# A chain of chunk states as one whole-array product for both heads, and small products set side by side in a decoder layer

## The chip, the cores and the metric

The kernel runs on one core of a Trainium2 chip. The metric is device time in microseconds (us) of one execution. A core has five engines that matter here: PE (matrix products; PEld is its loading of the stationary operand), DVE and ACT (elementwise work), POOL (small elementwise work) and SP (which only issues transfers). Each works through its own queue in order and waits for the others by semaphores.

## What is computed

One layer of a hybrid decoder on 512 tokens with 16 "meta" tokens ahead, 1024 channels, 16 heads of 64: sliding-window attention with sinks, beside it an RWKV-7 time mixing, the two merged by gates, a layer norm, a squared-ReLU MLP and a last norm. What matters for the change is the recurrence of the time mixing, per head with a 64x64 state S:

```
def step(S, inp):
    r_t, w_t, k_t, v_t, kk_t, a_t = inp
    sa = einsum('bhij,bhj->bhi', S, -kk_t)
    S = S * w_t[:, :, None, :] + sa[..., None] * (kk_t * a_t)[:, :, None, :] + v_t[..., None] * k_t[:, :, None, :]
    return S, einsum('bhij,bhj->bhi', S, r_t)
_, y = lax.scan(step, S0, (r, w, k, v, kk, a))
...
merged = sigmoid(gate_att) * att + sigmoid(gate_rwkv) * rw
h = layer_norm(ALPHA * h + merged @ w_out, ln1_g, ln1_b)
ff = square(relu(h @ w_ff1)) @ w_ff2
h = layer_norm(ALPHA * h + ff, ln2_g, ln2_b)
```

## The kernel before

Everything large is a dense product of float32 data that is split into a high and a low part (`whi`, `wlo`, `hhi`, `hlo`), so that three fast products (lines 340 to 342, tile `dps`) stand for one. A weight column block arrives by a transfer (`wraw`), ACT casts it to `whi` (line 256) and DVE subtracts to `wlo` (line 259). After the first norm come the input projections, 128 columns at a time, then the output projection (lines 1259 to 1261, tile `o`), then the MLP (lines 340 to 342 again, and 1485 to 1487, tile `acc`).

The 16 heads are taken as 8 pairs, one head in partitions 0 to 63 and the other in 64 to 127. The tokens of a pair are cut into 8 chunks of 64, and the recurrence becomes small float32 products: scores within a chunk (`sc`, line 658), an inverse that is built up block by block (`up`, lines 808, 817, 832, 842), its product with the keys (`wp`, line 859), the fold of everything that acts on the incoming state into one matrix per chunk (`gq`, line 876, added to `AX` by DVE at line 881), and then the chain: 7 steps in which chunk c's state is multiplied to give chunk c+1's. A step (`rwkv_chain`, line 936) was two products, one per head, each with 64 columns of the stationary operand `AX` and the 64 columns of that head's state `Z`, written to two different PSUM tiles (`ch`, `ch2`). `follow` then scales the two results by the chunk's decay into the next `Z`: head 0 on DVE (line 892), head 1 on ACT (line 894). The outputs of all chunks (`Y`, line 950) and their norm (`yt`, line 968) come behind the chain. The attention of a pair is scores (`sp`, line 1099; `copy_predicated`, bias and maximum on DVE, eight exponentials and eight scalings on ACT), transposes (`pt`, line 1143, copied to `pall` by ACT and `pown` by DVE) and the product with the values (`av`, line 1163). Low-rank products (`lps`, line 483), sums of squares (`ss`, line 564), gates (`gp`, line 1085), turned keys (`tr`), scores (`axt`) and values (`vt`) complete a pair.

All of this is laid between the dense products by hand. PE's order is that in which the code issues its instructions; the other engines' instructions are put in order by the framework, with priorities (`ahead`). The program goes through ten slots, one pair further each time: slot s does the scan preparation of pair s (`scan`), the solve and chain of pair s-1 (`solve`), the projections of pair s+1 (`project_in`), the attention of pairs s-1 and s-2 (`attend`, `attend_out`, `join`). Each item of a slot has a number, the time in us of dense work after which it is to come; `weave` sorts the items by it and issues dense products in portions of three (line 340 to 342) until the number is reached. PSUM tiles with the tag "a" (`sp`, `pt`, `av`, `lps`, `ss`, `gp`, `scm`, `bp`) share two banks, those with the tag "g" (`sc`, `axt`, `tr`, `vt`, `wp`, `gq`) two others, "ch" and "Y" one each, the dense products two.

Of the kernel before, what the change touches and what calls it, by code (L numbers as in the profile page):

```python
# [11 lines left out]
F32 = mybir.dt.float32  # L12
# [8 lines left out]
P = 128  # L21
# [7 lines left out]
HD = 64  # L29
C = 64  # L30
NCH = SEQ // C
PAIRS = HEADS // 2
# [98 lines left out]
def hybrid_layer_kernel(ctx: ExitStack, tc: tile.TileContext, I: dict, out: bass.AP):  # L131
# [12 lines left out]
    @contextmanager  # L144
    def ahead(n):

        now = tc.cur_priority
        tc.cur_priority = now - n
        yield
        tc.cur_priority += n  # L150
# [439 lines left out]
    def rwkv_bonus(j):  # L590
        S = SS[j]
        rkh, rkl = S["rk"]
        S["bv"] = dr.tile([P, SEQ], F32, name=f"bv{j}")
        bp = pat.tile([P, 512], F32, name="bp", tag="a")
        pe.matmul(bp, bones, rkh, start=True, stop=False)
        pe.matmul(bp, bones, rkl, start=False, stop=True)
        bv = ew.tile([P, SEQ], F32, name="bv", tag="rk")
        dve.tensor_tensor(bv, bp, S["v"][:, NMETA:], op=ALU.mult)
        nc.sync.dma_start(S["bv"], bv)
# [286 lines left out]
    def follow(S, c, src, last):  # L886

        Z, PC = S["Z"], S["PC"]
        for e in range(2):
            dst, scale = Z[c][ER[e], e, :], PC[ER[e], last : last + 1]  # L890
            if e == 0:
                dve.tensor_scalar(dst, src[e][ER[e]], scale, None, op0=ALU.mult)
            else:
                act.activation(dst, src[e][ER[e]], AF.Copy, scale=scale)  # L894
# [29 lines left out]
    def rwkv_chain(j, c):  # L924

        S = SS[j]
        Z, GQ = S["Z"], S["AX"]
        if c == 0:
            ch = pch.tile([P, 512], F32, name="ch", tag="ch", bufs=PS[2])

            ch2 = pch.tile([P, 512], F32, name="ch2", tag="Y", bufs=PS[3])
            S["st"] = [[b[:, d * C : (d + 1) * C] for b in (ch, ch2)] for d in range(NCH)]
        st = S["st"]
        with ahead(PRI["chain"]):
            for e in range(2):
                pe.matmul(st[c][e][ER[e]], GQ[:, c, 0, e, :], Z[c][:, e, :], start=True, stop=True)  # L936
            follow(S, c + 1, st[c], c)

    def rwkv_outputs(j):

# [413 lines left out]
    def scan(j):  # L1354

        need = (f"k{j}", f"r{j}", f"v{j}")
        return [
            (0.0, need, F(rwkv_scores, j, 0)),
            (3.2, (), F(rwkv_meta, j)),
            (3.2, (), F(rwkv_scores, j, 1)),  # L1360
            (3.2, (), F(rwkv_inverse, j)),
            (6.4, (), F(rwkv_bonus, j)),
            (12.55, (), F(rwkv_turn_scores, j)),
            (18.6, (), F(rwkv_turn_keys, j)),
            (16.0, (), F(rwkv_inverse_place, j)),
            (23.2, (), F(rwkv_turn_values, j)),
        ]

    def solve(j):

        return [
            (0.0, (), F(rwkv_blocks, j, 0)),
            (0.0, (), F(rwkv_start, j, 0)),
            (1.4, (), F(rwkv_blocks, j, 1)),
            (1.4, (), F(rwkv_start, j, 1)),
            (3.2, (), F(rwkv_blocks, j, 2)),
            (3.2, (), F(rwkv_start, j, 2)),
            (4.6, (), F(rwkv_blocks, j, 3)),
            (6.4, (), F(rwkv_turn_inverse, j)),
            (8.4, (), F(rwkv_fold, j, 0)),  # L1380
            (10.6, (), F(rwkv_fold, j, 1)),
        ] + [(11.6 + 0.95 * c, (), F(rwkv_chain, j, c)) for c in range(NCH - 1)] + [
            (18.6, (), F(rwkv_outputs, j)),
            (23.2, (), F(rwkv_norm, j)),
        ]

    def project_in(j):
        return [
            (0.0, (), F(rwkv_begin, j)),
            (8.4, (), F(rwkv_lora, j, 0)),  # L1390
            (10.6, (), F(rwkv_lora, j, 1)),
            (25.5 if j == 1 else 18.6, (f"k{j}",), F(rwkv_sums, j)),
        ]

    def attend(j, t0):
        return [
            (t0, (f"q{j}",), F(attention_scores, j, 0)), (t0 + 2.85, (), F(attention_scores, j, 1)),
        ]

    def attend_out(j, t0, t1, t2):  # L1400
        return [
            (t0, (), F(attention_turn, j, 0)),
            (t1, (), F(attention_out, j, 0)),
            (t1, (), F(attention_turn, j, 1)),
            (t2, (f"ga{j}",), F(attention_out, j, 1)),
        ]

    def join(j, t0, t1, t2):
        return [
            (t0, (f"gr{j}",), F(gate_out, j)), (t1, (), F(merge_rwkv, j)), (t2, (), F(merge, j)),  # L1410
        ]

    with tc.manual_schedule(engines={mybir.EngineType.PE}):
        for s in range(-1, PAIRS + 1):
            if s <= PAIRS:
                units[:] = [u for u in all_units[: marks[s + 1]] if u[0] not in finished]
            items = []
            if s > 0:
                items += solve(s - 1)
            if 0 <= s < PAIRS:  # L1420
                items += scan(s)
            if s == -1:
                items += [
                    (0.0, (), F(rwkv_begin, 0)),
                    (9.0, ("wa",), F(rwkv_lora, 0, 0)),
                    (10.4, (), F(rwkv_lora, 0, 1)),
                    (20.0, ("k0",), F(rwkv_sums, 0)),
                ]
            if 0 <= s < PAIRS - 1:
                items += project_in(s + 1)  # L1430
            if s == 0:
                items += [(18.0, ("av",), F(aside_heads, 0))]
            if s == 4:
                items += [(26.0, (), F(aside_heads, 1))]
            if s in (1, 5):
                items += [(8.6, (), turn_heads)]
            if 0 < s < PAIRS - 1:
                items += attend(s - 1, 12.55) + join(s - 1, 11.6, 25.4, 0)[:2]
            if 1 < s < PAIRS:

                items += attend_out(s - 2, 0.0, 4.6, 6.4) + join(s - 2, 0, 0, 7.0)[2:]
            if s == PAIRS - 1:
                items += [(10.0, (), merged_before)]
                items += attend(s - 1, 10.0) + attend_out(s - 1, 20.5, 22.9, 25.3)
                items += join(s - 1, 11.6, 26.5, 26.5)
                items += attend(s, 16.5)
                items += [(27.2, (), F(load_out, q, 0)) for q in range(3)]
            if s == PAIRS:
                items += attend_out(s - 1, 3.0, 5.4, 7.8) + join(s - 1, 0.0, 24.5, 25.5)
                items += [(2.0, (), F(merged, s - 2)), (25.6, (), F(merged, s - 1))]  # L1450
                items += [(3.0, (), residual_gain), (17.0, (), first_up)]
                items += [(3.0 + 3 * b, (), F(residual_rows, b)) for b in range(4)]
            weave(items, True)
# [261 lines left out]
```

## Time and profile before

| | |
|---|---|
| median of the runs | 972.86 us (971.6 to 973.08, 3 runs) |
| the profiled execution | 971.71 us, of which 969.9 us lie between its first and last instruction |
| busy share of the span | PE 97%, PEld 80%, DVE 65%, ACT 46%, POOL 5% |
| dense input projections and slots | about 60 to 580 us |
| MLP and end | about 580 to 970 us |

The page gives busy time, the span in 40 slices, the transfers, the chain of work that ended last, and groups of instructions with what they waited for. A timeline lists one engine's instructions in order of time: start, duration, engine, line, operation, tiles, rows*columns of the array that it uses, shape and count, and in brackets how long the engine was idle before it and who ended that. Matrix products are pipelined: the listed duration overlaps the next instruction, so what a product costs is read from the distance between starts.

### The profile page before, as it was taken

What the parts mean: (1) busy time and instruction counts of PE and PEld (TensorE: products, weight loads), DVE (VectorE), ACT (ScalarE), POOL (GpSimd) and SP (SyncE); (2) the same over time, 40 slices, a digit from 0 to 9 for tenths busy, and PEclk for the clock granted to TensorE, in tenths of its full rate; (3) what the DMA queues carried; (4) which work ended last, traced back from release to release, by engine and by line L of the source; (5) the groups of instructions that cost most, each with busy time, mean ns of one, the idle gap of its engine ahead of it and who ended that gap; (6) DMA issues with size and microseconds to landing.
All of it is one profiled execution on the core that took longest, in us unless ns stands there. A gap on an engine that the chain in (4) does not pass through costs nothing.

```text
span 969.9 us, 19424 instructions
## 1 busy us (share of the span) xinstructions
PE 942.1 (97%) x7805; PEld 775.6 (80%) x7805; DVE 633.1 (65%) x1444; ACT 447.7 (46%) x1111; POOL 44.3 (5%) x106
## 2 busy tenths in 40 slices
PE   4999999999999999999999999999999999999996
PEld 4888878788797887887876777988888888888885
DVE  8577788787887878868876948575423244542427
ACT  6536357475483664735727635643411224432220
POOL 2001000010000100000001000000000000000001
PEclk9999999999999999999999999999999999999999
DMA  7545323233322323142433725134223232232222
GB/s 271 94 126 129 85 70 93 65 75 91 91 81 82 92 78 92 47 118 74 129 93 90 234 88 216 55 121 130 87 88 107 88 107 90 86 106 90 83 91 87
DMA packets 79650, 99.95 MB, mean 103 GB/s; under 512 B 47174, under 2 KB 54072, under 8 KB 79560
## 3 DMA queue, kind: packets, MB, share of 16 engines
q1 hardware_dynamic: 78064, 96.63, 33.9%
q10 hardware_dynamic: 1496, 2.08, 0.6%
q8 instruction: 61, 1.00, 0.4%
q14 instruction: 29, 0.24, 0.1%
HBM read 85.23 MB, written 13.47 MB: 102 GB/s over the span
## 4 chain that ended last, share of the span: by engine, by line
PE 89%; DVE 5%; ACT 2%; DMA 2%; issue 1%; POOL 1%; SPq 0%; DVEq 0%; ACTq 0%; POOLq 0%
PE dps L340 17%; PE dps L341 15%; PE dps L342 15%; PE acc L1485 6%; PE acc L1486 6%; PE acc L1487 6%; PE av L1163 2%; PE sp L1099 2%; PE o L1259 2%; PE sc L658 2%; PE gq L876 2%; PE ch L936 1%; PE o L1260 1%; PE o L1261 1%; PE wp L859 1%; DVE wlo L259 1%
## 5 line engine op out<-in xcount | busy, mean ns | idle before, releaser
L259 DVE TENSOR_TENSOR wlo<-wraw,whi 128x512 fp32r<-128x512 f32 x240 | 157.1, 685 | 175.0 <-ACT whi L256 174.5
L256 ACT CAST whi<-wraw 128x512 fp32r<-128x512 f32 x240 | 139.8, 617 | 264.8 <-PE dps L341 117.5
L340 PE MATMUL dps<-hhi,whi 128*128 128x264 f32 (+1 forms) x640 | 218.5, 341 | 1.1 <-ACT whi L256 1.0
L341 PE MATMUL dps<-hlo,whi 128*128 128x264 f32 (+1 forms) x640 | 203.6, 318 | 0.9 <-DVE hlo L321 0.9
L342 PE MATMUL dps<-hhi,wlo 128*128 128x264 f32 (+1 forms) x640 | 203.1, 317 | 0.2 <-DVE wlo L259 0.2
L340 PEld LDWEIGHTS dps<-hhi,whi 128*128 128x128 f32 x640 | 120.4, 188 | 25.3 <-issue 14.6
L341 PEld LDWEIGHTS dps<-hlo,whi 128*128 128x128 f32 x640 | 120.8, 189 | 8.9 <-DVE hlo L321 1.7
L342 PEld LDWEIGHTS dps<-hhi,wlo 128*128 128x128 f32 x640 | 120.5, 188 | 8.8 <-DVE wlo L259 0.4
L341 PE MATMUL dps<-h1lo,whi 128*128 128x512 f32 (+1 forms) x256 | 97.3, 380 | 0.0
L340 PE MATMUL dps<-h1hi,whi 128*128 128x512 f32 (+1 forms) x256 | 97.3, 380 | 0.0
L342 PE MATMUL dps<-h1hi,wlo 128*128 128x512 f32 (+1 forms) x256 | 97.3, 380 | 0.0
L341 PEld LDWEIGHTS dps<-h1lo,whi 128*128 128x128 f32 x256 | 48.0, 188 | 10.3
L342 PEld LDWEIGHTS dps<-h1hi,wlo 128*128 128x128 f32 x256 | 48.0, 188 | 10.2
L340 PEld LDWEIGHTS dps<-h1hi,whi 128*128 128x128 f32 x256 | 48.0, 187 | 10.2
L1485 PE MATMUL acc<-whi,hhi 128*128 128x512 f32 x128 | 50.6, 395 | 0.0
L1486 PE MATMUL acc<-wlo,hhi 128*128 128x512 f32 x128 | 50.4, 394 | 0.0
L1487 PE MATMUL acc<-whi,hlo 128*128 128x512 f32 x128 | 50.2, 392 | 0.0
L1485 PE MATMUL acc<-whi,fhi 128*128 128x512 f32 x112 | 43.6, 389 | 0.0
L1486 PE MATMUL acc<-wlo,fhi 128*128 128x512 f32 x112 | 43.6, 389 | 0.0
L1487 PE MATMUL acc<-whi,flo 128*128 128x512 f32 x112 | 43.6, 389 | 0.0
L1585 DVE TENSOR_TENSOR rl<-rl 128x512 f32<-128x512 f32 (+1 forms) x36 | 22.7, 632 | 14.9 <-ACT hhi L1584 9.0
L894 ACT ACTIVATE Z<-ch,PC 64x64 f32<-64x64 f32 x56 | 17.3, 309 | 32.1 <-PE ch L936 31.3
(277 smaller groups left out, 1647.9 us busy)
## 6 DMA issues: line engine op xcount, KB each, us to landing
wraw<-in_w_ff_dram SPq DMA_DIRECT2D x64, 512.0 KB, 3.5
wraw<-in_w_in_dram SPq DMA_DIRECT2D x52, 512.0 KB, 3.6
wraw<-in_w_out_dram SPq DMA_DIRECT2D x8, 512.0 KB, 4.2
xt<-in_x_dram SPq DMA_DIRECT2D x4, 512.0 KB, 6.1
Nd<-NT SPq DMA_DIRECT2D x16, 128.0 KB, 2.9
bv<-bv SPq DMA_DIRECT2D x8, 256.0 KB, 2.7
bvm<-bv SPq DMA_DIRECT2D x8, 256.0 KB, 5.0
XB<-xtd SPq DMA_DIRECT2D x16, 128.0 KB, 3.2
```

Source lines behind the costliest of these rows:

```text
L256: act.copy(hi[:n, qs], raw[:n, qs])
L259: dve.tensor_tensor(lo[:n, qs], raw[:n, qs], hi[:n, qs].bitcast(F32), op=ALU.subtract)
L340: pe.matmul(ps, whi, xhi, start=first, stop=False)
L341: pe.matmul(ps, whi, xlo, start=False, stop=False)
L342: pe.matmul(ps, wlo, xhi, start=False, stop=last)
L658: pe.matmul(scs[d][to, c * P : (c + 1) * P], BK[ER[e], 4 * i + c, to], AXg[ER[e], e, 4 * i + c], start=True, stop=True,)
L876: pe.matmul(gqs[e][:, c * P : (c + 1) * P], WT[ER[e], 4 * i + c, :], GR[ER[e], 4 * i + c, :], start=True, stop=True,)
L1099: pe.matmul(sps[e][:, d * 256 : (d + 1) * 256], q[ER[e], n * P : (n + 1) * P], kk[ER[e], n * P : n * P + 256], start=True, stop=True,)
L1485: pe.matmul(acc[b], xhi[k][:, bs], hi[:, ws], start=first, stop=False)
L1486: pe.matmul(acc[b], xhi[k][:, bs], lo[:, ws], start=False, stop=False)
L1487: pe.matmul(acc[b], xlo[k][:, bs], hi[:, ws], start=False, stop=last)
L1585: dve.tensor_tensor(r, r, r, op=ALU.mult)
```

## The change

A chain step becomes one product for both heads: the stationary operand is all 128 columns of the chunk's `AX` (both heads), the moving one all 128 columns of `Z` (both heads), and the result is a 128x128 block. For each head `Z` holds the state in one half of the partitions and the chunk's values in the other, so that each head's product has all 128 rows, before as now; of the 128x128 result only the two diagonal 64x64 blocks are used, by `follow`. Four steps' results lie side by side in one PSUM tile: steps 0 to 3 in the "ch" tile, 4 to 6 in the "Y" tile, so that DVE's and ACT's halves of one step now stand in the same tile.

The numbers in the slots' lists are changed. Partial-array products (products that use 64 or fewer rows or columns of the array) of different origin now directly follow each other: the low-rank products `lps` come right behind `sc` and behind the meta step at the slot's start (they stood behind the two `gq` groups), attention scores behind the last block of the inverse and before `wp`, the value products `av` behind the two `gq` groups, the outputs `Y` behind `ss`. Chain steps begin earlier (10.4 in place of 11.6) and lie 1.25 apart in place of 0.95. The attention of a pair thereby moves: scores from 12.55 to 4.6, the transposes and value products of the pair before from 0.0 to 6.4 to 7.6 to 10.6. The start of a pair's low-rank work (`rwkv_begin`, a transfer of `lw`) is issued at the end of the slot before, and `bp` moves from the "a" banks to the "g" banks and a little earlier.

```diff
-        bp = pat.tile([P, 512], F32, name="bp", tag="a")
+        bp = pg.tile([P, 512], F32, name="bp", tag="g")
...
         if c == 0:
-            ch = pch.tile([P, 512], F32, name="ch", tag="ch", bufs=PS[2])
-            ch2 = pch.tile([P, 512], F32, name="ch2", tag="Y", bufs=PS[3])
-            S["st"] = [[b[:, d * C : (d + 1) * C] for b in (ch, ch2)] for d in range(NCH)]
-        st = S["st"]
+            S["ch"] = [
+                pch.tile([P, 512], F32, name="ch", tag=t, bufs=PS[b]) for t, b in (("ch", 2), ("Y", 3))
+            ]
+        ps = S["ch"][c // 4][:, c % 4 * P : (c % 4 + 1) * P]
         with ahead(PRI["chain"]):
-            for e in range(2):
-                pe.matmul(st[c][e][ER[e]], GQ[:, c, 0, e, :], Z[c][:, e, :], start=True, stop=True)
-            follow(S, c + 1, st[c], c)
+            pe.matmul(
+                ps, GQ[:, c, 0].rearrange("p e t -> p (e t)"), Z[c].rearrange("p e i -> p (e i)"),
+                start=True, stop=True,
+            )
+            follow(S, c + 1, [ps[:, e * HD : (e + 1) * HD] for e in range(2)], c)
...
-            (6.4, (), F(rwkv_bonus, j)),
+            (5.6, (), F(rwkv_bonus, j)),
...
-        ] + [(11.6 + 0.95 * c, (), F(rwkv_chain, j, c)) for c in range(NCH - 1)] + [
-            (18.6, (), F(rwkv_outputs, j)),
-            (23.2, (), F(rwkv_norm, j)),
+        ] + [(10.4 + 1.25 * c, (), F(rwkv_chain, j, c)) for c in range(NCH - 1)] + [
+            (18.61 + 0.6 * last, (), F(rwkv_outputs, j)),
+            (24.6 - 1.4 * last, (), F(rwkv_norm, j)),
...
-            (0.0, (), F(rwkv_begin, j)),
-            (8.4, (), F(rwkv_lora, j, 0)),
-            (10.6, (), F(rwkv_lora, j, 1)),
+        t0, t1 = (8.4, 10.6) if j == 1 else (0.0, 1.4)
+        begin = [(26.0, (f"k{j}",), F(rwkv_begin, j + 1))] if j < PAIRS - 1 else []
+        return begin + [
+            (t0, (), F(rwkv_lora, j, 0)),
+            (t1, (), F(rwkv_lora, j, 1)),
...
-                items += [(8.6, (), turn_heads)]
+                items += [(2.4, (), turn_heads)]
...
-                items += attend(s - 1, 12.55) + join(s - 1, 11.6, 25.4, 0)[:2]
+                items += attend(s - 1, 4.6, 1.8) + join(s - 1, 13.5, 25.4, 0)[:2]
...
-                items += attend_out(s - 2, 0.0, 4.6, 6.4) + join(s - 2, 0, 0, 7.0)[2:]
+                items += attend_out(s - 2, 7.6, 8.4, 9.4, 10.6) + join(s - 2, 0, 0, 11.6)[2:]
...
-                items += attend(s - 1, 10.0) + attend_out(s - 1, 20.5, 22.9, 25.3)
+                items += attend(s - 1, 4.6, 1.8) + attend_out(s - 1, 15.6, 16.6, 16.6, 18.0)
...
-                items += attend(s, 16.5)
+                items += attend(s, 11.6, 2.2)
```

Three places show what this does to the queues; the rows are the built programs' order, with the shape of the result and a count.

First, PE in the middle of a slot, in the chain. `axt` is the turning of the scores, `sp` the attention scores. Before:

```order
L936 MATMUL ch<-Z,AX 64x64
L936 MATMUL ch_3488<-Z,AX 64x64
L694 MATMUL axt<-con,AX 128x128 x8
L1099 MATMUL sp<-kk,q 128x256 x4
L340 MATMUL dps<-hhi,whi 128x264
```

and now:

```order
L694 MATMUL axt<-con,AX 128x128 x8
L340 MATMUL dps<-hhi,whi 128x264
L341 MATMUL dps<-hlo,whi 128x264
L342 MATMUL dps<-hhi,wlo 128x264
L936 MATMUL ch<-Z,AX 128x128
```

The two products of a step are one, the turning stands by itself between dense products, and the attention scores have left the chain.

Second, PE at the fold (`gq`) ahead of the chain. Before:

```order
L876 MATMUL gq<-GR,WT 128x128 x8
L483 MATMUL lps<-zz,lw 128x264 x2
L340 MATMUL dps<-hhi,whi 128x512
L341 MATMUL dps<-hlo,whi 128x512
L342 MATMUL dps<-hhi,wlo 128x512
```

and now:

```order
L342 MATMUL dps<-hhi,wlo 128x512
L936 MATMUL ch<-Z,AX 128x128
L876 MATMUL gq<-GR,WT 128x128 x8
L1166 MATMUL av<-pall,vtok 64x128 x2
L1166 MATMUL av<-pown,vdif 64x128 x2
```

The low-rank products behind the fold have given way to the value products, and the first chain step stands ahead of the second half of the fold. The low-rank products now stand in the run of small products at the slot's start, behind `sc`, and behind the meta step.

Third, ACT between the later chain steps, with what each instruction waits for (`Z<-ch` is ACT's half of `follow`). Before:

```order
L894 ACTIVATE Z<-ch_4359,PC 64x64 [waits PE_49] x3
L256 CAST whi<-wraw 128x512 [waits DMAHW0_49,PE_49]
L421 ACTIVATE k<-dps,drv 128x264 [waits PE_49]
L256 CAST whi<-wraw 128x512
L894 ACTIVATE Z<-ch_4359,PC 64x64 [waits PE_49]
```

and now:

```order
L894 ACTIVATE Z<-ch,PC 64x64 [waits DVE_49] x2
L256 CAST whi<-wraw 128x512 [waits DMAHW1_49,PE_49]
L421 ACTIVATE k<-dps,drv 128x264 [waits PE_49]
L894 ACTIVATE Z<-ch,PC 64x64 [waits DVE_49]
L256 CAST whi<-wraw 128x512
```

ACT's half of a step waited for PE's product; now, with both halves in one PSUM tile, it waits for DVE's half.

More of the change, by code (lines that the diff above doesn't have):

```diff
@@ L1369, in solve @@
     def solve(j):
+        last = j == PAIRS - 1
         return [
@@ L1381, in solve, with attend, attend_out @@
             (10.6, (), F(rwkv_fold, j, 1)),
-        ] + [(11.6 + 0.95 * c, (), F(rwkv_chain, j, c)) for c in range(NCH - 1)] + [
-            (18.6, (), F(rwkv_outputs, j)),
-            (23.2, (), F(rwkv_norm, j)),
+        ] + [(10.4 + 1.25 * c, (), F(rwkv_chain, j, c)) for c in range(NCH - 1)] + [
+            (18.61 + 0.6 * last, (), F(rwkv_outputs, j)),
+            (24.6 - 1.4 * last, (), F(rwkv_norm, j)),
         ]
     def project_in(j):
-        return [
-            (0.0, (), F(rwkv_begin, j)),
-            (8.4, (), F(rwkv_lora, j, 0)),
-            (10.6, (), F(rwkv_lora, j, 1)),
+        t0, t1 = (8.4, 10.6) if j == 1 else (0.0, 1.4)
[3 more added lines that the diff above has]
+            (t1, (), F(rwkv_lora, j, 1)),
             (25.5 if j == 1 else 18.6, (f"k{j}",), F(rwkv_sums, j)),
         ]
-    def attend(j, t0):
+    def attend(j, t0, dt=3.6):
         return [
-            (t0, (f"q{j}",), F(attention_scores, j, 0)), (t0 + 2.85, (), F(attention_scores, j, 1)),
+            (t0, (f"q{j}",), F(attention_scores, j, 0)), (t0 + dt, (), F(attention_scores, j, 1)),
         ]
-    def attend_out(j, t0, t1, t2):
+    def attend_out(j, t0, t1, t2, t3):
         return [
@@ L1403, in attend_out @@
             (t1, (), F(attention_out, j, 0)),
-            (t1, (), F(attention_turn, j, 1)),
-            (t2, (f"ga{j}",), F(attention_out, j, 1)),
+            (t2, (), F(attention_turn, j, 1)),
+            (t3, (f"ga{j}",), F(attention_out, j, 1)),
         ]
@@ L1427, in hybrid_layer_kernel @@
                     (20.0, ("k0",), F(rwkv_sums, 0)),
+                    (24.0, ("k0",), F(rwkv_begin, 1)),
                 ]
@@ L1435, in hybrid_layer_kernel @@
             if s in (1, 5):
-                items += [(8.6, (), turn_heads)]
+                items += [(2.4, (), turn_heads)]
             if 0 < s < PAIRS - 1:
-                items += attend(s - 1, 12.55) + join(s - 1, 11.6, 25.4, 0)[:2]
+                items += attend(s - 1, 4.6, 1.8) + join(s - 1, 13.5, 25.4, 0)[:2]
             if 1 < s < PAIRS:
-                items += attend_out(s - 2, 0.0, 4.6, 6.4) + join(s - 2, 0, 0, 7.0)[2:]
+                items += attend_out(s - 2, 7.6, 8.4, 9.4, 10.6) + join(s - 2, 0, 0, 11.6)[2:]
             if s == PAIRS - 1:
-                items += [(10.0, (), merged_before)]
-                items += attend(s - 1, 10.0) + attend_out(s - 1, 20.5, 22.9, 25.3)
-                items += join(s - 1, 11.6, 26.5, 26.5)
-                items += attend(s, 16.5)
+                items += [(14.0, (), merged_before)]
+                items += attend(s - 1, 4.6, 1.8) + attend_out(s - 1, 15.6, 16.6, 16.6, 18.0)
+                items += join(s - 1, 15.0, 26.5, 26.5)
+                items += attend(s, 11.6, 2.2)
                 items += [(27.2, (), F(load_out, q, 0)) for q in range(3)]
             if s == PAIRS:
-                items += attend_out(s - 1, 3.0, 5.4, 7.8) + join(s - 1, 0.0, 24.5, 25.5)
+                items += attend_out(s - 1, 3.0, 5.4, 5.4, 7.8) + join(s - 1, 0.0, 24.5, 25.5)
                 items += [(2.0, (), F(merged, s - 2)), (25.6, (), F(merged, s - 1))]
```

## The prediction

> **What bounds the kernel now.** I read the page's busy times and the chain that ended last, then PE's timeline in one slot, then what PE waited for.
>
> ```profile
> PE 942.1 (97%) x7805; PEld 775.6 (80%) x7805; DVE 633.1 (65%) x1444; ACT 447.7 (46%) x1111; POOL 44.3 (5%) x106
> PE 89%; DVE 5%; ACT 2%; DMA 2%; issue 1%; POOL 1%; SPq 0%; DVEq 0%; ACTq 0%; POOLq 0%
> ```
>
> PE is busy for 97% of the span and holds 89% of the chain that ended last, so what PE's row of products costs is nearly what the program costs. But a busy PE is not one that streams all the time: its recorded durations overlap, and the price of a group lies in the distance between starts. I price every group in one way: from the start of the dense product ahead of it to the start of the second dense product behind it, less two dense products at their usual distance. The second one is taken because the first behind a group starts early on paper and then stays long.
>
> A chain step between dense products, in PE's timeline of the slot at 300 to 345 us:
>
> ```profile
> 324.87 0.28 PE L341 MATMUL dps<-hlo,whi 128*128 128x264 f32 x1
> 324.99 0.28 PE L342 MATMUL dps<-hhi,wlo 128*128 128x264 f32 x1
> 325.20 0.34 PE L936 MATMUL ch<-Z,AX 128*64 128x64 f32 x4
> 325.47 0.39 PE L340 MATMUL dps<-hhi,whi 128*128 128x264 f32 x1
> 325.69 0.28 PE L341 MATMUL dps<-hlo,whi 128*128 128x264 f32 x1
> ```
>
> Dense products of 264 columns start 0.12 apart (324.87, 324.99). The step's two products (four passes, float32 takes two each) reach from 324.99 to 325.69: 0.70, less 0.24, is **0.46 us**. The passes themselves are short. The rest is seen at the edges: 0.21 in place of 0.12 from the dense product to the step, and 0.22 in place of 0.12 behind it.
>
> A float32 product of the whole array, 128 columns, shows no such edges. The nearest row is the turning of the values, four products of two passes:
>
> ```profile
> 95.29 0.28 PE L342 MATMUL dps<-hhi,wlo 128*128 128x264 f32 x1
> 95.41 1.05 PE L732 MATMUL vt<-con,v 128*128 128x128 f32 x8
> ...
> 96.43 0.28 PE L341 MATMUL dps<-hlo,whi 128*128 128x264 f32 x1
> ```
>
> 1.14 less 0.24 is 0.90 for eight passes, 0.112 each with nothing left over for the edges (128 columns at the dense pace of 264 in 0.12 would be 0.06 a pass, so float32 streams at about half that pace).
>
> **The change part by part.** *The chain step.* One product of two passes at 0.112 is 0.22, against 0.46: 0.24 less. Of 56 steps (7 in each of 8 pairs) that is **-13.2**. Bounds: if a short whole-array group pays the edges after all, 0.22+0.20 leaves about 0.04 per step, -2; more than -13.2 can't be had, since 0.112 a pass is what PE streams. I take -13.2, as the row of four products leaves no remainder.
>
> The Trainium skill speaks against this step: TensorEngine Tiling (Array Packing), Overview, has half-width products run side by side for up to twice the speed, so a full product that computes two unused blocks would give that away. The trace agrees as far as the streaming goes (two heads' passes cost 0.11 there, 0.22 here); by that rule alone the change would cost 56 x 0.11 = 6 us, an estimate from these rows. The same page's Tiling Modes section says that a change of tiling mode drains the array, and the 0.46 holds both the gain and the drains, so that this rule is no rival here.
>
> *The small products side by side.* What a pairing saves depends on the two shapes, and the trace has a pair of like shape and one of unlike shape, each with its members alone:
>
> ```profile
> 310.45 0.39 PE L342 MATMUL dps<-hhi,wlo 128*128 128x512 f32 x1
> 310.77 1.16 PE L876 MATMUL gq<-GR,WT 64*128 64x128 f32 x16
> 311.76 0.61 PE L483 MATMUL lps<-zz,lw 64*128 64x264 f32 x4
> ...
> 312.65 0.39 PE L341 MATMUL dps<-hlo,whi 128*128 128x512 f32 x1
> ```
> ```profile
> 498.73 0.39 PE L342 MATMUL dps<-hhi,wlo 128*128 128x512 f32 x1
> 499.05 1.16 PE L876 MATMUL gq<-GR,WT 64*128 64x128 f32 x16
> ...
> 500.47 0.40 PE L341 MATMUL dps<-hlo,whi 128*128 128x512 f32 x1
> ```
> ```profile
> 76.58 0.39 PE L341 MATMUL dps<-hlo,whi 128*128 128x512 f32 x1
> 76.81 0.40 PE L342 MATMUL dps<-hhi,wlo 128*128 128x512 f32 x1
> 77.14 0.72 PE L483 MATMUL lps<-zz,lw 64*128 64x264 f32 x4
> ...
> 78.13 0.40 PE L341 MATMUL dps<-hlo,whi 128*128 128x512 f32 x1
> ```
>
> Dense products of 512 columns start 0.23 apart (76.58, 76.81), so two are 0.46. Fold and low-rank products together (both 64*128): 2.20 less 0.46 is 1.74 here; alone they are 1.28 and 0.86, together 2.14. A pair of like shape saves **0.40**.
>
> ```profile
> 138.93 0.28 PE L342 MATMUL dps<-hhi,wlo 128*128 128x264 f32 x1
> 139.14 0.34 PE L936 MATMUL ch<-Z,AX 128*64 128x64 f32 x4
> 139.41 1.13 PE L1099 MATMUL sp<-kk,q 64*128 64x256 f32 x8
> ...
> 140.70 0.28 PE L341 MATMUL dps<-hlo,whi 128*128 128x264 f32 x1
> ```
> ```profile
> 501.41 0.40 PE L342 MATMUL dps<-hhi,wlo 128*128 128x512 f32 x1
> 501.74 1.14 PE L1099 MATMUL sp<-kk,q 64*128 64x256 f32 x8
> ...
> 503.14 0.40 PE L341 MATMUL dps<-hlo,whi 128*128 128x512 f32 x1
> ```
>
> A chain step (128*64) and attention scores (64*128) together: 1.77 less 0.24 is 1.53; alone 0.46 and 1.27, together 1.73. A pair of unlike shape saves **0.20**: one change of shape where there were two, while like shapes save both. (The skill's rule on modes, named above, would give just this ratio.)
>
> Now the ledger, by the order of the change. Lost: 12 pairs of fold and low-rank products (like, 4.8), 6 of chain step and scores (1.2), 6 of inverse and value products (unlike, 1.2): 7.2. Gained: 7 of inverse and scores, 6 of `sc` and low-rank, 6 of the meta step and low-rank, 12 of fold and value products, all unlike, 31 x 0.20 = 6.2; 6 of sums and outputs (`ss`, `Y`: 128*64 both, with one product of 16 columns between; 0.2 to 0.4, I take 0.3) 1.8: 8.0. The gathering is worth **-0.8**, between -2 and +0.5: it dissolves the one kind of pair that saved double.
>
> *Waits removed.* Attention scores now stand far from `gp`, behind which they had to find a free "a" bank:
>
> ```profile
> 256.87 0.28 PE L342 MATMUL dps<-hhi,wlo 128*128 128x264 f32 x1
> 257.08 0.34 PE L936 MATMUL ch<-Z,AX 128*64 128x64 f32 x4
> 257.35 1.09 PE L694 MATMUL axt<-con,AX 128*128 128x128 f32 x8
> 258.37 1.67 PE L1099 MATMUL sp<-kk,q 64*128 64x256 f32 x8
> ...
> 260.20 0.28 PE L341 MATMUL dps<-hlo,whi 128*128 128x264 f32 x1
> ```
>
> 3.33 less 0.24 is 3.09, where the parts are 0.46, 0.90 (eight passes of a transpose, as above) and 1.27, 2.63: 0.5 is waiting, in the five slots that show it **-2.5** (bounds 0 and -3.5). Two single waits stand near other moved items:
>
> ```profile
> 124.11 0.50 PE L1033 MATMUL vp<-con,vT 64*128 64x64 f32 x5 [0.66 <-ACT tw L487]
> PE pt L1143 <- DVE sb L1106: 1.5, 1, 1.5
> ```
>
> The turning of the attention's values (`vp`, twice) waited 0.66 behind the low-rank products and now stands alone: it saves the waits, about 1.3, and pays both edges, 0.4 each: **-0.5**. The 1.5 is in the last attention, whose transposes now stand 9.2 units behind the scores in place of 7.65: half of it, **-0.7** (0 to -1.5).
>
> *Waits added.* ACT's half of a step now follows DVE's. Before, they ran side by side:
>
> ```profile
> 326.75 0.34 PE L936 MATMUL ch<-Z,AX 128*64 128x64 f32 x4
> 327.12 0.28 DVE L892 TENSOR_SCALAR Z<-ch,PC 64x64 f32<-64x64 f32 x1 [0.63 <-PE ch L936]
> 327.16 0.31 ACT L894 ACTIVATE Z<-ch,PC 64x64 f32<-64x64 f32 x1 [1.19 <-PE ch L936]
> ```
>
> From product to scale 0.37, and 0.05 more for 128 columns in the last pass; then 0.28 on DVE and 0.31 on ACT one after the other, with 0.1 for handing over (an estimate): 1.1 us from one step's start to the earliest start of the next. In the change's order the tightest links have nine dense products between, 9 x 0.12 + 0.22 = 1.32, two in a slot, then twelve (1.68); the others have 1.9 or more. So the new wait is covered with 0.2 to spare on the tight ones, as long as neither engine is just busy with something else; a cast `whi` or a DVE sum is 0.6 to 0.7 long. Queued behind in ACT are the casts that later dense products need, with a whole dense unit in hand. I take half of the 16 tight links late by 0.4: **+3.2** (0 to 6.4).
>
> The moved `lw` transfer is issued a slot's end earlier, on SP, and its buffer is free since the slot's start; `bp` needs a "g" bank between `sc` and `wp`, both long read: nothing for either; a late "g" bank would cost one DVE mask, 0.7, per slot.
>
> **Sum:** -13.2 - 0.8 - 0.5 - 2.5 - 0.7 + 3.2 = -14.5. The profiled execution took 971.71 (span 969.9), so 957.2 like it; the median of the runs is 1.15 above, 972.86, so **958.4**. The one forecast's own range, from the terms' bounds, is 954 to 963.
>
> **Rivals.**
> (a) *Unlike shapes save as much as like ones.* Then 31 gained pairs are worth 0.4 and 12 lost unlike ones too: 6.2 - 2.4 = 3.8 more, 954.6; with the sums' pair at 0.4 some 954. Against it stands the row at 139 us.
> (b) *The attention's softmax gets in the way.* Its eight exponentials now run on ACT in the stretch of the fold, ahead of the copy `pall` that the value products wait for:
>
> ```profile
> 339.13 0.40 ACT L1127 ACTIVATE sb<-sb,nm 128x128 f32<-128x128 f32 x1
> 339.52 0.40 ACT L1127 ACTIVATE sb<-sb,nm 128x128 f32<-128x128 f32 x1
> ```
>
> Eight at 0.39 are 3.1, and a copy of 128x512 about 0.6: 3.7 from when the run begins. Between the second transposes and their value products PE has six dense products, a chain step and a fold, 1.4 + 0.2 + 1.1 = 2.7. If they coincide, value products start 1.0 late in 6 slots: +6, 964.4. For it: all of it is in ACT's order. Against: the run must begin just as the transposes end.
> (c) *The short full product gains nothing*, edges and all: the chain's 13.2 is lost, 971.6, no change that can be told.
> (d) *Slower: the serial halves stall the chain.* If at every tight link a DVE sum (0.68) and an ACT cast (0.62) stand ahead of the two halves, a step needs 2.4: late by 1.08, 1.08 and 0.72 at the links of 1.32, 1.32 and 1.68, 2.9 a slot, 23 in eight; 958.4 - 3.2 + 23 = 978.2. It decides from 17.7 us, 0.37 on each of 48 links. For it: DVE is busy 65% of the span. Against: the program puts the chain's halves ahead by the largest priority, and dense products give each link the slack above.
>
> **How the numbers follow.** Forecast 0.76, (a) 0.08, (b) 0.09, (c) 0.03, (d) 0.04. The range 953 to 964.5 leaves out (c), (d) and the tails of the others, some 15 to 20%. A change of under 0.2% (1.9 us) can't be told from none. Faster: forecast, (a) and (b), 0.93; same: (c), 0.03; slower: (d), 0.04.
>
> **What would show it.** Chain step between dense products: 0.46 becomes 0.22, and dense products around it 0.12 apart; the line's passes fall from 224 to 112. Fold and value products should cost 0.2 less together than apart. `Z` on ACT should start right behind `Z` on DVE, and PE's waits for ACT's `Z` come to 0 to 6 us. It is wrong if step edges stay, if PE waits long for `Z` or `pall`, or if the slots shorten by much less than 1.8 us each (14.5 over eight).

## The result, and the profile after

The changed kernel took 965.92 us (median of 4 runs, 964.21 to 967.13) beside 972.23 for the kernel before on the same chip: ratio 0.9934, interval 0.9914 to 0.9955. It is faster, by 6.3 us, where 14.5 were forecast; 965.92 lies above the range. The profiled execution took 965.14 in place of 971.71, so it shows the same difference (6.6).

The page of the changed kernel, its busy times and the shares of the chain that ended last:

```profile
PE 931.8 (97%) x7693; PEld 776.7 (81%) x7693; DVE 631.0 (66%) x1444; ACT 449.9 (47%) x1111; POOL 43.7 (5%) x106
PE 78%; DVE 13%; ACT 4%; DMA 2%; issue 2%; POOL 1%; SPq 0%; DVEq 0%; ACTq 0%; POOLq 0%
```

PE is still the bound, with 112 passes fewer (7805 to 7693); a pass is one MATMUL record, and a float32 product has two. But its share of the chain that ended last fell from 89% to 78%, and DVE's rose from 5% to 13%: for some stretches something else now sets the time.

PE's timeline of the changed kernel, the last five chain steps of one slot, each with the dense products beside it:

```profile
320.11 0.28 PE L342 MATMUL dps<-hhi,wlo 128*128 128x264 f32 x1
320.23 0.39 PE L936 MATMUL ch<-Z,AX 128*128 128x128 f32 x2
...
322.28 0.28 PE L342 MATMUL dps<-hhi,wlo 128*128 128x264 f32 x1
322.83 0.49 PE L936 MATMUL ch<-Z,AX 128*128 128x128 f32 x2 [0.27 <-ACT Z L894]
...
324.50 0.28 PE L342 MATMUL dps<-hhi,wlo 128*128 128x264 f32 x1
324.63 0.38 PE L936 MATMUL ch<-Z,AX 128*128 128x128 f32 x2
324.76 0.37 PE L340 MATMUL dps<-hhi,whi 128*128 128x264 f32 x1
324.97 0.28 PE L341 MATMUL dps<-hlo,whi 128*128 128x264 f32 x1
...
325.95 0.38 PE L936 MATMUL ch<-Z,AX 128*128 128x128 f32 x2
...
327.13 0.28 PE L342 MATMUL dps<-hhi,wlo 128*128 128x264 f32 x1
327.54 0.49 PE L936 MATMUL ch<-Z,AX 128*128 128x128 f32 x2
```

By the prediction's way of pricing, the undisturbed step at 324.63 costs 324.97 - 324.50 - 0.24 = 0.23, in place of 0.46. Into the step it is now 0.13 in place of 0.21. The 0.21 between the two dense products behind it has stayed, but the whole is no more than two passes at 0.11 take, so nothing is left over for edges. Two of the five don't start 0.12 behind their dense product, though: the fourth of the slot's seven steps (322.83) starts 0.55 behind it, 0.43 late, and the seventh (327.54) 0.41 behind it, 0.29 late. The same stands in slot after slot: 0.43 late at five fourth steps and 0.29 at another, 0.29 at six seventh steps and one third step, and 0.18 at one more of each, which stand behind dense products of 512 columns. A late step also pushes the dense product behind it by 0.1 (priced as a group, the one at 322.83 costs 0.53 more than the undisturbed one, the one at 327.54 0.39 more). All in all that is 6.2 us, against 0.7 before (two steps).

Summed over all groups between dense products from 75 to 640 us, again with that price, the groups took 228.7 us before and 221.0 after, 7.7 less, and the dense products 1.1 more. Of what the chain's steps gave up (13.3), the waits took back about 5.5.

### The profile page after: what moved, and what is told of

It reads as the page before. It is cut to its first block, busy times and chain, and to the rows that moved or that the text cites. A ratio compares the mean times of both kernels' runs of the same rounds, so it can differ in the third digit from the quotient of the medians.

```text
span 963.3 us, 19229 instructions
## 1 busy us (share of the span) xinstructions
PE 931.8 (97%) x7693; PEld 776.7 (81%) x7693; DVE 631.0 (66%) x1444; ACT 449.9 (47%) x1111; POOL 43.7 (5%) x106
## 4 chain that ended last, share of the span: by engine, by line
PE 78%; DVE 13%; ACT 4%; DMA 2%; issue 2%; POOL 1%; SPq 0%; DVEq 0%; ACTq 0%; POOLq 0%
PE dps L340 14%; PE dps L341 13%; PE dps L342 13%; PE acc L1492 6%; PE acc L1493 6%; PE acc L1494 6%; DVE wlo L259 2%; DVE ftmp L761 2%; PE sp L1102 2%; DVE Xf L765 2%; PE sc L658 2%; DVE AX L881 2%; PE wp L859 1%; PE o L1262 1%; PE o L1263 1%
## 5 line engine op out<-in xcount | busy, mean ns | idle before, releaser
L340 PEld LDWEIGHTS dps<-hhi,whi 128*128 128x128 f32 x640 | 120.5, 188 | 22.3 <-issue 11.6
```

Of the source, the lines that this page charges most:

```text
L340: pe.matmul(ps, whi, xhi, start=first, stop=False)
```

## The experiments

All kernels compute the whole layer. Times are medians; the ratio is to the kernel before, timed with it on the same chip.

| kernel | time | before | ratio | interval |
|---|---|---|---|---|
| chain product alone, old order | 974.31 | 971.57 | 1.0029 | 1.0017 to 1.0041 |
| new order alone, old chain step | 970.46 | 971.57 | 0.9990 | 0.9981 to 0.9999 |
| two whole-array products per step | 970.23 | 971.57 | 0.9986 | 0.9977 to 0.9994 |
| identity's copies on ACT | 966.96 | 971.57 | 0.9953 | 0.9941 to 0.9965 |
| both scalings on DVE | 969.62 | 971.56 | 0.9978 | 0.9968 to 0.9988 |
| identity's copies written later | 965.79 | 971.56 | 0.9937 | 0.9925 to 0.9949 |
| the last two edits together | 969.70 | 971.56 | 0.9979 | 0.9969 to 0.9989 |
| old order, chain product, both scalings on DVE | 979.04 | 971.56 | 1.0080 | 1.0063 to 1.0098 |
| one copy held back by data | 963.55 | 972.0 | 0.9911 | 0.9898 to 0.9924 |
| both scalings on DVE into the seventh step | 966.28 | 972.0 | 0.9938 | 0.9926 to 0.9951 |
| the last two edits together | 964.72 | 972.0 | 0.9923 | 0.9910 to 0.9936 |
| both copies held back by data | 962.87 | 971.9 | 0.9905 | 0.9891 to 0.9918 |
| the changed kernel again | 965.24 | 971.9 | 0.9928 | 0.9914 to 0.9941 |

### The chain's product and the order, each alone

The first kernel has the new `rwkv_chain` and the old lists of numbers, the second the new lists and the old `rwkv_chain`.

```diff
 e1: (11.6 + 0.95 * c, (), F(rwkv_chain, j, c))   one whole-array product
 e2: (10.4 + 1.25 * c, (), F(rwkv_chain, j, c))   two half-width products
```

> The kernel before with the chain step alone changed (one whole-array product, results in one PSUM tile); the slots' tables stay as they were. Theory (the product saves 0.24 us in each of 56 steps, and waits of PE for the next state give part of it back): a chain step between dense products costs 0.22 where PE does not wait, and the time is 962 to 967 us, 6 to 10 below the kernel before. Rival (the new tables make the whole difference): within 1 us of the kernel before, 971 to 973. If the time is below the changed kernel's 965.9, the tables cost time.

> The changed kernel with the old chain step (two half-width products into two PSUM tiles); the new tables alone. Theory (pairs of unlike shape save 0.2, so that gained and lost pairs cancel): within 3 us of the kernel before, 969 to 973, PE's wait for the next state shorter than in the changed kernel, since the two halves run side by side. Rival (every pair saves 0.4): 7 us below the kernel before, 965.

The second came out as expected: 970.46, no wait of PE for `Z`, a chain step at 0.46 to 0.47 between dense products. The first did not, by either theory: 2.8 us slower than before. What PE and its weight loads waited for in that kernel (us in total, times, longest):

```profile
PE ch L936 <- ACT Z L894: 8.4, 21, 1.1
...
PEld ch L936 <- ACT Z L894: 15.2, 25, 1.3
```

And one link of it, in the timelines of DVE, ACT and PE:

```profile
319.36 1.28 DVE L881 TENSOR_TENSOR AX<-AX,gq 128x512 f32<-128x512 f32 x2
...
320.87 0.27 DVE L892 TENSOR_SCALAR Z<-ch,PC 64x64 f32<-64x64 f32 x1
```
```profile
321.17 0.31 ACT L894 ACTIVATE Z<-ch,PC 64x64 f32<-64x64 f32 x1 [2.35 <-DVE Z L892]
```
```profile
318.18 0.38 PE L936 MATMUL ch<-Z,AX 128*128 128x128 f32 x2
...
321.53 0.49 PE L936 MATMUL ch<-Z,AX 128*128 128x128 f32 x2 [1.02 <-ACT Z L894]
```

The product starts at 318.18, DVE comes to its half only at 320.87, behind the sums of `AX`, and ACT, idle for 2.35 us, may not begin before DVE is done. Before, ACT did not wait for DVE. So the chain's product takes 13 us off PE and loses more than that to waits at the steps, in this order. The one-after-the-other is only a part of this link's wait: DVE's half ends at 321.14 and ACT's at 321.48, so 0.34 is ACT's standing behind, and the rest is that DVE itself comes late. Over the whole kernel the steps start late by 12.5 us in all; if each had waited for DVE's half alone, about 4 would be left (an estimate from the timelines). The order alone is worth 1.1 us (its interval ends just below 1). Together they are worth 6.3, some 8 more than the sum of the two (2.8 slower and 1.1 faster): the new order's main worth is that it makes room for the new product's chain, not the pairs of small products. Whether the wider spacing does this, or the work that no longer stands ahead of the halves in DVE's and ACT's queues, these two runs don't separate.

### Two tiles, so that the halves run side by side

```diff
-            pe.matmul(ps, GQ[:, c, 0] (both heads), Z[c] (both heads), ...)
-            follow(S, c + 1, [ps[:, e * HD : (e + 1) * HD] for e in range(2)], c)
+            for e in range(2):
+                pe.matmul(st[c][e], GQ[:, c, 0] (both heads), Z[c][:, e, :], ...)
+            follow(S, c + 1, st[c], c)
```

> The changed kernel, but each chain step is two whole-array products, all 128 columns of AX with the 64 state columns of one head, into two PSUM tiles, so that ACT's half no longer waits for DVE's. Theory (the serial halves make the wait of 0.29 at the last chain step of a slot): ACT's half starts with DVE's and that wait goes, 2 us; if four passes of 64 columns cost what two of 128 do (0.22) the time is 963 to 964. Rival (a pass of 64 columns is bound by its weight load, 0.11 like one of 128): a step costs 0.44, the time is 974 to 977.

In this kernel's timelines, a step, the dense products about it and the two halves:

```profile
324.67 0.28 PE L342 MATMUL dps<-hhi,wlo 128*128 128x264 f32 x1
324.79 0.55 PE L936 MATMUL ch<-Z,AX 128*128 128x64 f32 x4
325.15 0.37 PE L340 MATMUL dps<-hhi,whi 128*128 128x264 f32 x1
325.35 0.29 PE L341 MATMUL dps<-hlo,whi 128*128 128x264 f32 x1
...
326.70 0.55 PE L936 MATMUL ch<-Z,AX 128*128 128x64 f32 x4
```
```profile
327.07 0.28 DVE L892 TENSOR_SCALAR Z<-ch,PC 64x64 f32<-64x64 f32 x1 [0.97 <-PE ch L936]
```
```profile
327.29 0.31 ACT L894 ACTIVATE Z<-ch,PC 64x64 f32<-64x64 f32 x1 [1.61 <-PE ch L936]
```

ACT's half now waits for PE and overlaps DVE's, and every wait of PE for `Z` is gone: steps start 0.12 behind dense products of 264 columns and 0.23 behind those of 512, as an undisturbed step does. This shows that the waits come from the two halves of one tile. A step that takes 0.2 longer also leaves the halves 0.2 more time, but at the seventh step that isn't needed: in the trace of this slot both halves end 0.5 or more before its product starts. At the fourth, DVE's half ends only 0.19 before it, so that some 0.1 might have been left with the shorter step (an estimate). But the step costs 325.35 - 324.67 - 0.24 = 0.44: four passes at 0.11, so 64 moving columns cost as much as 128 (0.11 a pass there too). What the waits gave back, the passes took: 970.23, which is in neither range, since the waits went as the theory said and the step costs what the rival said.

### What makes the fourth step late

In the changed kernel, DVE and POOL ahead of the fourth step, whose product could only start at 322.83:

```profile
319.36 0.68 DVE L1187 TENSOR_TENSOR z<-z,ga 128x512 f32<-128x512 f32 x1
319.96 0.18 DVE L765 TENSOR_TENSOR Xf<-Xf,ftmp 66x39 f32<-66x39 f32 x1
320.18 0.56 DVE L761 TENSOR_TENSOR ftmp<-Xf,Nf 66x28 f32<-66x28 f32 x1
320.77 0.63 DVE L765 TENSOR_TENSOR Xf<-Xf,ftmp 66x28 f32<-66x28 f32 x1
321.44 0.17 DVE L761 TENSOR_TENSOR ftmp<-Xf,Nf 66x15 f32<-66x15 f32 x1
...
322.16 0.27 DVE L892 TENSOR_SCALAR Z<-ch,PC 64x64 f32<-64x64 f32 x1
```
```profile
320.09 1.28 POOL L702 COPY AX<-con 64x512 f32<-64x512 f32 x2 [6.67 <-PE axt L694]
```

Two operations of 66x28 take 0.56 and 0.63, the one of 66x39 ahead of them 0.18. Both read two SBUF tiles, and both lie beside POOL's two copies of the identity (0.64 each, from 320.09): the first ends at 320.74 and the second at 321.40, each about when a copy does. The rule is in the Trainium skill, SBUF — State Buffer, Who interferes with whom: a VectorE (DVE) instruction with two SBUF inputs contends with a GpSimd (POOL) instruction that reads SBUF; the ports that they share are an exclusive lock, and the order of issue decides which of the two is blocked. The trace agrees, 0.18 becoming 0.56 and 0.63; the prediction had not looked for it. In this slot of the kernel before, the same copies ran at 321.19, beside an operation with one PSUM operand (0.67, as elsewhere) and a copy that took 0.48 in place of 0.37.

Four kernels move the copies. The first gives them to ACT:

```diff
-                pool.tensor_copy(
+                act.copy(
                     AXg[R, e, :, 0, :], ident[R, R].unsqueeze(1).to_broadcast([HD, NCH, C])
```

> The changed kernel, but the two copies of the identity into AX, which POOL makes behind the turned scores, are made by ACT. Theory (POOL's copies hold up two small DVE operations, 0.56 and 0.63 in place of 0.18, and through them DVE's half of the third chain step): those two operations take 0.18, PE's wait of 0.43 at the fourth step goes, 2.6 us in six slots, less what two more copies of 0.4 to 0.6 in ACT's queue cost: 963 to 966. Rival (the DVE queue is late for another reason): the wait stays, 966 or more.

The sums fall to 0.18, but the fourth step is still 0.25 late, now because one of the copies (0.62) stands ahead of ACT's half; the fifth becomes 0.30 late in ACT's longer queue, and the seventh stays 0.29 late: 966.96, no gain. The second writes the copies further down in the program, in `rwkv_turn_keys`:

> The changed kernel, with GpSimd's copies of the identity written in the program behind the chain in place of ahead of it. Theory (these copies stretch VectorE's sums of two SBUF operands from 0.18 to 0.6 beside the chain's fourth step): the sums take 0.18 to 0.3 there, the wait of 0.43 before six of the fourth steps goes, 2.6 us less, 963 to 964. Rival (the copies only fall on other VectorE work with the same worth): the wait turns up elsewhere, 965 to 967.

It tests nothing, since POOL is idle and the framework puts the copies where they were (the trace of this kernel):

```profile
319.53 1.28 POOL L707 COPY AX<-con 64x512 f32<-64x512 f32 x2 [6.67 <-PE axt L694]
```

They are released by `axt` after the same 6.67 us of idling, with everything else 0.56 earlier too. So it is a repetition of the changed kernel, and its 965.79 is one. The third and fourth hold them back by data: they read a copy of the identity of which ACT rewrites a column from the fourth chain product (times zero, plus the identity).

```diff
+        if c == 3 and j < PAIRS - 1:
+            act.activation(idt[:, 0:1], ps[:, 0:1], AF.Identity, bias=ident[:, 0:1], scale=0.0)
+            place_ident(j + 1)        # the two pool.tensor_copy, reading idt
```

> The changed kernel, with GpSimd's copies of the identity held back by data: they read a copy of the identity of which ScalarE rewrites one column from the fourth chain product, so they can't start before it. Theory (the copies stretch VectorE's two-operand sums ahead of the fourth step's scaling): beside no copy these sums take 0.18 to 0.2 in place of 0.56 and 0.63, VectorE's scaling is 0.8 earlier, the wait of 0.43 before six of the fourth steps goes, 2.6 less by the steps and about 1.2 more for ScalarE's new operations if they delay anything: 963 to 965. Rival (the fourth step waits for the long chain of VectorE work ahead, with or without the copies): the wait stays above 0.3 and the time at 965 to 967.

The rewritten column lies in one head's half of the identity, so one copy was held back and the other still ran at its old place, which makes this run the better test. DVE and POOL in this kernel:

```profile
319.15 0.18 DVE L773 TENSOR_TENSOR Xf<-Xf,ftmp 66x39 f32<-66x39 f32 x1
319.37 0.63 DVE L769 TENSOR_TENSOR ftmp<-Xf,Nf 66x28 f32<-66x28 f32 x1
320.04 0.18 DVE L773 TENSOR_TENSOR Xf<-Xf,ftmp 66x28 f32<-66x28 f32 x1
```
```profile
319.36 0.61 POOL L710 COPY AX<-idt 64x512 f32<-64x512 f32 x1 [6.74 <-PE axt L694]
```

One copy, one stretched operation. The fourth step starts 0.17 behind its dense product in place of 0.55, in five slots, and the time is 963.55, as the theory expected. With a column rewritten in both halves:

> As the run with the identity's copies held back, but both copies are held (there one of the two still ran at its old place, since the rewritten column lay in the other's half): ScalarE rewrites one column in each half from the fourth product. Theory (each copy beside VectorE stretches one of its two-operand sums): with one copy left one sum took 0.63, with none left none is above 0.2, and the fourth step's entry falls from 0.17 to 0.12; 0.3 us less by the steps, 0.15 to 0.26 more per slot on ScalarE, which has time there: 962.5 to 964. Rival (ScalarE's second rewriting delays its next scaling): 964 to 966.

> The changed kernel itself, unaltered, beside the run with both copies held. Theory (the fourth step's wait is worth its 0.38 in six slots): 1.5 to 3.5 us above that run, 965 to 967. Rival (the gain in the slots is given back elsewhere, and the two medians differed by chance): within 1 us of it.

```profile
318.85 0.18 DVE L769 TENSOR_TENSOR ftmp<-Xf,Nf 66x28 f32<-66x28 f32 x1
319.07 0.18 DVE L773 TENSOR_TENSOR Xf<-Xf,ftmp 66x28 f32<-66x28 f32 x1
```
```profile
320.95 0.28 PE L342 MATMUL dps<-hhi,wlo 128*128 128x264 f32 x1
321.07 0.38 PE L944 MATMUL ch<-Z,AX 128*128 128x128 f32 x2
```

Nothing is stretched, and the fourth steps that were late by 0.43 and 0.29 are on time (here at 321.07, 0.12 behind the dense product). Set instruction by instruction against the changed kernel's trace, PE gains 0.55 in each of five slots (0.43 at the step, the rest at the products behind it), 2.9 by the sixth. Measured: 962.87 beside 965.24 for the changed kernel on the same chip, 2.4, and the slowest run of the one (963.64) is faster than the fastest of the other (964.28). Each is as its theory expected. The intervals (0.9891 to 0.9918 and 0.9914 to 0.9941) share a hair's breadth; 963.55 for the one held copy, against 965.79 and 965.92 for the changed kernel, all timed apart, says the same. This is the fastest kernel here.

### What makes the seventh step late

ACT in the changed kernel, ahead of the seventh step; its product could only start at 327.54:

```profile
326.02 0.62 ACT L256 CAST whi<-wraw 128x512 fp32r<-128x512 f32 x1 [0.36 <-PE dps L341]
326.67 0.48 ACT L421 ACTIVATE k<-dps,drv 128x264 f32<-128x264 f32 x1
327.18 0.31 ACT L894 ACTIVATE Z<-ch,PC 64x64 f32<-64x64 f32 x1
```

DVE's half had started at 326.37 and took 0.28, so ACT could have begun at 326.67; it did the copy first and began at 327.18. Five kernels give ACT's half to DVE, in the whole chain or at this link alone:

```diff
-            if e == 0:
+            if e == 0 or c == 6:        # at the one link; elsewhere always
                 dve.tensor_scalar(dst, src[e][ER[e]], scale, None, op0=ALU.mult)
```

> The changed kernel, with both scalings of a chain step on VectorE (none on ScalarE). Theory (the waits at the chain's sixth and seventh steps come from ScalarE's queue, where a cast of 0.62 and a copy of 0.48 stand ahead of its half; the wait at the fourth step comes from VectorE and stays): the wait of 0.29 before seven of the later steps goes, 2 us less, 963 to 965, and the wait of 0.43 at the fourth step stays. Rival (VectorE, busy for 65% of the span, is the nearer limit: each link now holds two of its operations of 0.28, and a sum ahead of them delays both): new waits at other links, 966 or more.

The seventh steps start 0.12 behind their dense product in the middle slots, so their lateness was ACT's queue. But the fourth ones become worse:

```profile
325.41 0.28 PE L342 MATMUL dps<-hhi,wlo 128*128 128x264 f32 x1
326.84 0.49 PE L933 MATMUL ch<-Z,AX 128*128 128x128 f32 x2 [1.15 <-DVE Z L891]
```

1.43 in place of 0.55: both halves now stand behind DVE's sums, and the time is 969.62. The rival was right. Next, the same edit on the old order:

> The order of the kernel before, with the one whole-array product per step and both scalings on VectorE. With the scalings on two engines this order took 974.3, with 8.4 us of waits for ScalarE's Z and more at the weight loads. Theory (ScalarE's queue behind VectorE's makes these waits): they shrink to less than half, 964 to 970. Rival (the order's link of 0.95 is shorter than any serial pair of scalings, and VectorE's sum of 1.28 and scan of 1.24 stand ahead): waits stay of the same size, 971 to 976.

It takes 979.04, above both ranges. With the scalings on two engines, steps of the middle slots were late at the second, fourth and seventh place (by some 0.8, 0.4 and 0.4). Now the fourth and seventh are on time, so those were ACT's queue; the second stays 0.8 late, which is DVE's. The waits at the steps alone become shorter, by about 4 us, but DVE, with twice the halves, makes others wait:

```profile
PE ch L933 <- DVE Z L891: 5.7, 10, 0.9
...
PE Y L950 <- DVE Z L891: 2.2, 6, 0.4
PE sp L1099 <- DVE gg L1087: 2.0, 6, 0.4
```

Priced as groups, those with `Y` and with `sp` cost 2.1 and 2.8 more than with two engines, and those with the inverse and `sc` 3.0, of which 1.8 in one place (at 174 us), where the granted clock fell as well. So the theory was right for ACT's part of the waits, and the rival named DVE's; neither priced the waits elsewhere.

> The two edits together: the identity's copies behind the chain and both scalings on VectorE. Theory (two separate causes): their gains add, 961 to 962.5, and TensorE waits for Z for less than 1.5 us in all. Rival (VectorE's queue takes what ScalarE's loses): 964 to 967.

The kernel of both edits, with 969.70, is the one with both scalings on DVE (969.62) again, since writing the copies later moves nothing. At the one link alone:

> The changed kernel, with both scalings on VectorE at one link alone, that into the seventh step, where ScalarE has a cast of 0.62 and a copy of 0.48 ahead. Theory (that wait is ScalarE's queue, and elsewhere two engines are better than one): the seventh step's 0.29 goes in seven slots and nothing else moves, 2 us less, 963.5 to 964.5. Rival (what the link gains the dense product behind it waits for, as VectorE's own work moves): 965 to 966.5.

The seventh step's 0.29 goes in six slots, and PE's list of waits has a new line:

```profile
PE dps L340 <- ACT q L1054: 1.0, 6, 0.2
```

PE comes earlier to a dense product that needs the bank which ACT's copy of `q` frees; set against the changed kernel, each slot gains 0.28 at the seventh step and loses 0.31 to 0.36 at that product. The wait has moved, not gone: 966.28, the rival's.

> The changed kernel with both: the identity's copies held back by the fourth product and both scalings on VectorE at the link into the seventh step. Theory (two separate causes of the chain's waits): the gains add, 961 to 963, and TensorE waits for Z only in the second and last slots. Rival (the scheduler or the queues give it back): 964 to 967.

964.72 for this and the held copy together, against 963.55 for the held copy alone: the gains don't add, since the second one isn't one.

## Why the prediction was wrong

**The chain step was right**: 0.46 became 0.23, the passes 224 became 112, nothing is left for the edges; -13.3 in products, as forecast (-13.2). Rival (c) is out, and so are the 6 us that the prediction worked out as a cost of the two unused blocks. (Its 0.11 for the two heads' passes is no reading: by its own rows 0.46 less the two edges is 0.27, and 32 passes of that shape, the outputs `Y`, cost 1.29 between dense products, 0.16 for four.)

**The price of a pair was right.** A group of fold and value products, in the changed kernel:

```profile
309.33 0.40 PE L342 MATMUL dps<-hhi,wlo 128*128 128x512 f32 x1
309.65 1.16 PE L876 MATMUL gq<-GR,WT 64*128 64x128 f32 x16
...
312.11 0.39 PE L341 MATMUL dps<-hlo,whi 128*128 128x512 f32 x1
```

312.11 - 309.33 - 0.46 is 2.32, apart 1.28 and 1.22: 0.19 saved. The other unlike pairs save 0.20 to 0.21, so rival (a) is out. The sums with the outputs were over-sized: the group with the turned keys costs 3.32, only 0.14 less than the same products in their earlier order (3.46), where 0.3 was taken. The ledger comes to 0 in place of -0.8. `vp`, standing alone, costs 1.09 and 1.15 and still waits for `tw` (0.8 in two), so it gives nothing in place of -0.5.

**The step that failed is the one on added waits**, and it failed in two places. The first is its term at the chain's steps, "half of the 16 tight links late by 0.4: +3.2". Its link time was right: the product at 324.63, DVE's half at 325.05, ACT's at 325.36 for 0.31, the next product possible some 0.1 later, 1.1 us. So, nearly, was its guess at the tight links: of the two in a slot, that into the sixth step (1.32, to 325.95) is on time and that into the seventh is late, 2.6 us in all, though the chain's priority was to prevent it: ACT did a copy first. What failed is that it took the slack from the dense products between steps and called links of 1.9 and more safe. The link into the fourth step has 2.17 and is late, because DVE reaches its half 1.9 us after the product, behind the sums that POOL's copies stretch; the fourth steps make 3.0 us and two third ones 0.6. At the chain's steps it comes to 6.2 us (0.7 stood there before), near the upper bound of 6.4. By itself this would have given about 961, inside the range. The second place is waits that the sum put at nothing: for the moved work it had asked only whether buffers (`lw`, `bp`) come free. They make 3.2 more, some 964, and three small gains that did not come (`vp`, the pairs, the wait at `pt`, 2.0 together) carry the time out of the range.

**Waits that weren't in the sum.** The wait at `sp` went as forecast (-2.5). But others came with the moved work, in PE's list of the changed kernel:

```profile
PE dps L340 <- DVE k L415: 1.4, 1, 1.4
...
PE up L832 <- DVE X L827: 1.2, 2, 1.0
...
PE sp L1102 <- DVE ga L1172: 0.8, 1, 0.8
```

The second stands in the last attention's stretch, where the forecast was that half of `pt`'s 1.5 would go (-0.7): the inverse (`up`) takes its place, 1.45 there in all. The third is part of 1.5 in the slot of the last scores, `gp` adds 0.6, and the first 1.1 at a dense product, 3.2 together. In the kernel with the new order and the old chain step the same three stand at much the same size (0.7, 0.3 and 1.7 in its list, where the changed kernel has 0.8, 0.3 and 1.4): they come with the order, not with the chain's product.

The account, forecast and measured, in us:

| term | forecast | measured |
|---|---|---|
| chain product | -13.2 | -13.3 |
| pairs | -0.8 | 0 |
| `vp` | -0.5 | 0 |
| waits at `sp` | -2.5 | -2.5 |
| wait at `pt`, now at `up` | -0.7 | 0 |
| waits at the chain's steps, over the 0.7 before | +3.2 | +5.5 |
| waits not foreseen | 0 | +3.2 |
| sum | -14.5 | -7.1 |

The profiled executions differ by 6.6. The table leaves out some 0.7 of cost at the transposes `pt`, which stand alone in twelve places and cost 0.05 to 0.07 less beside other small products before; the rest is smaller still.

**The rivals.** (b) did not come: PE's list has no wait for `pall`. (d), the serial halves stalling the chain, was the right mechanism, at a quarter of its price in this order (6.2 of 23, and more than half of it at links that it didn't name); in the old order it is decisive, together with DVE's own lateness, 2.8 us slower than before. It was given 0.04.

**What stays open.** Whether the fourth step would stay on time if the copies weren't there at all and ACT weren't used was not tried. The 3.2 us of waits that weren't in the sum were read from the traces, and no run takes them away. What part of the new order makes room for the chain, its wider spacing or the work that it moves, was not tested apart.

## What to carry to other kernels

When two engines' halves of a step come to read one tile, the link becomes a chain through both queues: price it by when each engine reaches its half, read in its own timeline, and not by the bound engine's slack. A change that shortens a step of a recurrence is worth what the spacing of the steps allows; here product and order were worth 2.8 us less than nothing and 1.1 us alone, and 6.3 together. Before moving work, look what POOL does beside it: here two short copies in each slot cost 2.4 us through VectorE's two-operand sums.

## What the runs showed that was not expected

A float32 pass with 64 moving columns and a whole-array stationary operand took 0.11 us, as long as one with 128 (0.44 for four, 0.23 for two); what bounds it there was not tested. In the profiled executions of five of these runs (the last five of the table), the granted clock fell for some microseconds in the last slot with a chain, near PE's wait at `up`. The same stretch (its length, busy us of PE, PEld, DVE, ACT and POOL, the granted clock, the share and rate of transfers) in the changed kernel and in its repetition:

```profile
538.00:548.00 10.00, 8.83 (x115) 6.75 (x114) 9.94 (x18) 3.78 (x11) 0.00 (x0) 1.00 0.74 282
```
```profile
538.00:548.00 10.00, 8.83 (x107) 6.59 (x106) 8.93 (x16) 3.02 (x8) 0.00 (x0) 0.83 0.72 268
```

It came in some executions of the same kernel and not in others, and what sets it off was not tested; all five are the runs profiled on two of the chips, and none of the eight profiled on two others shows it in this stretch, though one of these (old order, both scalings on DVE) has a fall to 0.83 between 170 and 180 us; so whether it is a matter of the chip stays open too. 10 us at 0.83 are at most 1.7 us of lost time, and at the lowest, 0.72, 2.8 (estimates), as much as the held copies are worth, so these are judged by the medians of all runs and not by two profiled executions.
